# Products of one weight unit: all eight with the high parts, then all eight with the low parts

## The chip, the cores and the metric

The kernel runs on one NeuronCore of a Trainium2 chip. The metric is the device time of one execution in microseconds (us). An engine is named as in the profile: PE multiplies matrices, PEld is its weight load (which can run beside a product), DVE and ACT work on vectors, POOL does a few odd jobs, SP issues the DMAs.

## The reference

A two-layer encoder over 256 frames and a width of 2048. What matters here are the products with large weight matrices, all in float32:

```python
u = rms_norm(h, a_norm_g);  proj = u @ a_w_in          # q, k, v and a forget gate
h = h + forgetting_attention(q, k, v, logf) @ a_w_out
h = h + relu(rms_norm(h, g) @ w1)**2 @ w2              # 2048 -> 8192 -> 2048
kv = rms_norm(h, kv_norm_g) @ kv_w                     # shared keys and values
q = rms_norm(rms_norm(h, b_norm_g) @ b_w_q)            # layer 2: own queries
h = h + chunked_relbias_attention(q, k, v, rel) @ b_w_out
h = h + relu(rms_norm(h, g) @ w1)**2 @ w2
```

## The kernel before

**Split operands.** Weights and activations are split into a high part (rounded to the type `fp32r`) and a low part (the rest). A product of two such numbers is formed as high x high + high x low + low x high; low x low is left out. An activation tile `x[k]` holds the high parts of 128 features of all 256 frames in columns 0 to 255 and their low parts in columns 256 to 511.

**Units.** The weights stream from memory in 768 units of 128 x 1024 numbers (512 KB). For each, `issue` has SP start a DMA into `raw` (L94, 4 buffers), ACT write `hi` (L96, 3 buffers) and DVE write `lo = raw - hi` (L97, 3 buffers). `fetch` keeps two units ahead of the one that is handed out.

**Two ways to use a unit.** In `panel_a` (192 units: queries, keys and values of both layers) the activations are the stationary operand and the weights stream through as the moving one: twelve products of 512 columns for each unit (L179 to L181). In `panel_b` (576 units: both output projections and both MLPs) the weights are stationary. A unit holds four row blocks (`j`) of two 128-column blocks (`i`). `unit_b` forms, for each of these eight tiles, a pair:

- L191: `hi` tile stationary, all 512 columns of `x[k]` moving. The result, 128 x 512, goes to the accumulator bank `ps[i]`.
- L192: the `lo` tile of the same place stationary, the 256 high columns of `x[k]` moving, added to the first 256 columns of the same bank.

Every product is preceded by a load of its own 128 x 128 stationary tile, so a unit has 16 loads and 16 products. Below, L191's products are called wide and L192's narrow.

**Panels.** Four units fill the two banks `ps[0]`, `ps[1]` of a panel (16 values of `k`). There are four accumulator banks, so in the MLPs the next panel has two banks of its own; the output projections take two panels together (`group=2`) and use all four. A finished bank goes to `evac`: `residual` (L228, L229, both DVE), or `act` of the MLP (L389 to L396, ACT and DVE), after which it may be overwritten. The last panel of all ends in `store`, which adds to `h` and sends it out (L448).

**Order on the engines.** The tile framework fixes each engine's instruction order when the kernel is built, and adds the semaphore waits. After each unit `run_fill` takes one entry of a list of small jobs (attention, the sums for the norms); `Stats.reduce` at L149 is one, four products with only 2 moving columns.

Of the kernel before, what the change touches and what calls it, by code (L numbers as in the profile page):

```python
# [15 lines left out]
P = 128  # L16
T = 256
NB = T // P
D = 2048
KT = D // P  # L20
# [10 lines left out]
UB = UN // 256  # L31
# [4 lines left out]
def trunk(ctx: ExitStack, tc: tile.TileContext, xT, gs, hg, bf, wgate, w_in, w_oa, w1a, w2a,  # L36
          w_kv, w_qb, w_ob, w1b, w2b, rel, out):
    nc = tc.nc
    V, S, G, TE = nc.vector, nc.scalar, nc.gpsimd, nc.tensor
# [67 lines left out]
    def run_fill():  # L107
        if fill:
            for f in fill.popleft():
                f()  # L110
# [73 lines left out]
            evac(b, ps[b])  # L184

    def unit_b(ps, hi, lo, x, u):
        for i in range(2):
            for j in range(UB):
                k = u * UB + j
                c = j * 256 + i * P  # L190
                TE.matmul(ps[i], hi[:, c : c + P], x[k], start=k == 0, stop=False)  # L191
                TE.matmul(ps[i][:, :T], lo[:, c : c + P], x[k][:, :T], start=False, stop=k == KT - 1)  # L192
        run_fill()

    def panel_b(x, evac, n, group=1):
        for n0 in range(0, n, group):
            ps = [[ps_acc.tile([P, 512], F32, name="acc") for _ in range(2)] for _ in range(group)]
            for u in range(KT // UB):
                for q in range(group):
                    hi, lo = fetch()  # L200
                    unit_b(ps[q], hi, lo, x, u)
            for q in range(group):
                for i in range(2):
                    evac(2 * (n0 + q) + i, ps[q][i])
# [75 lines left out]
    def qkv_tile(name):  # L280
        return qkv.tile([P, GH, T], F32, name=name)
# [5 lines left out]
            else:  # L287
                fill.append(it)

# [1 line left out]
    st0 = Stats("a")  # L291
    x = []

# [78 lines left out]
    for g in range(NG):  # L372
        q, k, v = qkv.tile([P, GH, T], F32, name="q", bufs=4), qkv_tile("k"), qkv.tile([P, NB, 512], F32, name="v")
# [40 lines left out]
    st2f = st2.flip()  # L414
    add_fill([[], [lambda: st2.reduce(True)], [lambda: st2f.reduce(True)]])

# [1 line left out]
    qs = []  # L418
    for g in range(NG):
        q = qkv.tile([P, GH, T], F32, name="q", bufs=4)  # L420
# [13 lines left out]
    for g in range(NG):  # L434
        k, v = qkv_tile("k"), qkv.tile([P, NB, 512], F32, name="v")
# [73 lines left out]
```

## Time and profile before

| | before |
|---|---|
| time, median of 3 runs | 2217.13 us (2215.26 to 2217.21) |
| profiled execution, first to last instruction | 2213.9 us |
| PE busy | 2207.1 us |
| PEld busy | 1911.9 us |
| DVE busy | 1371.1 us |
| ACT busy | 1097.4 us |
| granted PE clock | 1.000 |
| wide products L191 | 4608, 392 ns each as recorded |
| narrow products L192 | 4608, 280 ns each as recorded |
| loads of both | 9216, 187 and 189 ns each as recorded |

The profile gives for the profiled execution only its span, 2213.9 us; the median of the runs is 3.2 us above it, which is taken as what lies around the span. Products overlap: a recorded duration runs from a product's start to the modelled end of its last result, while the next product has long begun. What one product costs is therefore read from start to start, and is called its slot below.

### The profile page before, as it was taken

To read this page: it belongs to the slowest core of one execution; us is meant where nothing else is said; L and a number is where in the kernel's file an instruction comes from. 1 tells how busy PE (TensorE), PEld (TensorE's weight loads), DVE (VectorE), ACT (ScalarE), POOL (GpSimd) and SP (SyncE) were. 2 spreads that over 40 slices of the span, in tenths; PEclk is the share of its full clock that TensorE was granted. 3 is DMA by queue.
4 is the path that set the end of the run, shared out by engine and by line. 5 is a ranking of instruction groups with operands and counts; after the bars stand their busy time and mean duration, and the time that the engine had idled before them with its cause. 6 is when DMAs were issued, how large, how long until landed. Compare 5 with 4: busy or idle time off the path is not lost.

```text
span 2213.9 us, 31170 instructions
## 1 busy us (share of the span) xinstructions
PE 2207.1 (100%) x12084; PEld 1911.9 (86%) x12084; DVE 1371.1 (62%) x2011; ACT 1097.4 (50%) x1578; POOL 42.5 (2%) x53
## 2 busy tenths in 40 slices
PE   9999999999999999999999999999999999999999
PEld 7888888888888888888888888888888888888888
DVE  6665557665665566566765555667656655655665
ACT  5554555553454454355554555545534534544543
POOL 1000000000000000000000000000000000000000
PEclk9999999999999999999999999999999999999999
DMA  6555555555555555555555555455555555555564
GB/s 224 206 182 173 179 178 184 190 191 190 191 190 191 190 191 190 190 190 190 190 183 184 178 173 170 162 190 190 190 189 189 189 190 190 190 189 189 190 205 155
DMA packets 118819, 414.32 MB, mean 187 GB/s; under 512 B 13312, under 2 KB 19600, under 8 KB 118672
## 3 DMA queue, kind: packets, MB, share of 16 engines
q1 hardware_dynamic: 118672, 412.34, 56.5%
q8 instruction: 94, 1.54, 0.3%
q14 instruction: 53, 0.43, 0.1%
HBM read 410.17 MB, written 2.12 MB: 186 GB/s over the span
## 4 chain that ended last, share of the span: by engine, by line
PE 98%; DMA 1%; DVE 0%; ACT 0%; issue 0%; SPq 0%; POOL 0%; ACTq 0%; DVEq 0%
PE acc L191 47%; PE acc L192 25%; PE acc L179 8%; PE acc L181 8%; PE acc L180 8%; PE s L234 1%; PE po L262 1%; PE pt L223 1%; DMA raw<-in_w_in 0%; PE pt L256 0%; PE s L233 0%; PE po L263 0%; DMA bias<-cd 0%; PE s L331 0%; DVE lo L97 0%
## 5 line engine op out<-in xcount | busy, mean ns | idle before, releaser
L191 PE MATMUL acc<-act,hi 128*128 128x512 f32 x4608 | 1599.4, 392 | 0.0
L97 DVE TENSOR_TENSOR lo<-raw,hi 128x1024 fp32r<-128x1024 f32 (+1 forms) x770 | 938.3, 1221 | 730.4 <-ACT hi L96 729.1
L96 ACT ACTIVATE hi<-raw 128x1024 fp32r<-128x1024 f32 (+1 forms) x770 | 815.5, 1059 | 1028.3 <-PE acc L191 769.3
L192 PE MATMUL acc<-act,lo 128*128 128x256 f32 x4608 | 1288.6, 280 | 0.0
L191 PEld LDWEIGHTS acc<-act,hi 128*128 128x128 f32 x4608 | 862.0, 187 | 189.8
L192 PEld LDWEIGHTS acc<-act,lo 128*128 128x128 f32 x4608 | 870.3, 189 | 0.0
L179 PE MATMUL acc<-hi,act 128*128 128x512 f32 x768 | 311.1, 406 | 1.3 <-ACT act L120 1.1
L180 PE MATMUL acc<-lo,act 128*128 128x512 f32 x768 | 299.4, 390 | 0.6 <-DVE lo L97 0.5
L181 PE MATMUL acc<-hi,act 128*128 128x512 f32 x768 | 299.9, 391 | 0.0
L181 PEld LDWEIGHTS acc<-hi,act 128*128 128x128 f32 x768 | 144.0, 188 | 31.8 <-DVE act L121 0.5
L180 PEld LDWEIGHTS acc<-lo,act 128*128 128x128 f32 x768 | 144.5, 188 | 29.7 <-DVE lo L97 2.0
L179 PEld LDWEIGHTS acc<-hi,act 128*128 128x128 f32 x768 | 144.4, 188 | 29.6 <-ACT act L120 1.9
L229 DVE TENSOR_TENSOR h<-acc,h 128x256 f32<-128x256 f32 x160 | 67.0, 423 | 4.9
L228 DVE TENSOR_TENSOR h<-acc,h 128x256 f32<-128x256 f32 x160 | 65.8, 415 | 5.2 <-PE acc L192 5.2
L389 ACT ACTIVATE tb<-acc 128x256 f32<-128x256 f32 x128 | 47.9, 374 | 29.3 <-PE acc L192 29.3
L395 ACT ACTIVATE act<-a 128x256 fp32r<-128x256 f32 x128 | 52.7, 412 | 2.0
L390 DVE TENSOR_TENSOR tb<-acc,tb 128x256 f32<-128x256 f32 x128 | 53.4, 417 | 0.1
L396 DVE TENSOR_TENSOR act<-a,act 128x256 fp32r<-128x256 f32 x128 | 53.4, 418 | 0.0
L393 ACT ACTIVATE a<-tb 128x256 f32<-128x256 f32 x128 | 51.4, 401 | 0.0
L216 DVE TENSOR_TENSOR qn<-acc,rn 128x512 f32<-128x512 f32 x32 | 22.1, 691 | 37.4 <-POOL rn L214 37.4
L120 ACT ACTIVATE act<-h,gsb 128x256 fp32r<-128x256 f32 x80 | 38.6, 496 | 6.9 <-DVE h L229 6.8
L214 POOL TENSOR_TENSOR rn<-vv,mhalf 128x4 f32<-128x4 f32 x32 | 32.7, 1021 | 404.6 <-DVE vv L212 404.6
(113 smaller groups left out, 603.0 us busy)
## 6 DMA issues: line engine op xcount, KB each, us to landing
raw<-in_w1a SPq DMA_DIRECT2D x128, 512.0 KB, 3.3
raw<-in_w2a SPq DMA_DIRECT2D x128, 512.0 KB, 3.3
raw<-in_w1b SPq DMA_DIRECT2D x128, 512.0 KB, 3.3
raw<-in_w2b SPq DMA_DIRECT2D x128, 512.0 KB, 3.6
raw<-in_w_in SPq DMA_DIRECT2D x94, 512.0 KB, 3.4
raw<-in_w_kv SPq DMA_DIRECT2D x64, 512.0 KB, 3.4
raw<-in_w_oa SPq DMA_DIRECT2D x32, 512.0 KB, 4.2
raw<-in_w_qb SPq DMA_DIRECT2D x32, 512.0 KB, 3.3
```

The lines of the kernel that those rows point to most:

```text
L96: S.activation(hi[:, c], raw[:, c], AF.Copy)
L97: V.tensor_tensor(lo[:, c], raw[:, c], hi[:, c].bitcast(F32), op=ALU.subtract)
L179: TE.matmul(ps[b], xh, wh, start=k == 0, stop=False)
L180: TE.matmul(ps[b], xh, wl, start=False, stop=False)
L181: TE.matmul(ps[b], xl, wh, start=False, stop=k == KT - 1)
L191: TE.matmul(ps[i], hi[:, c : c + P], x[k], start=k == 0, stop=False)
L192: TE.matmul(ps[i][:, :T], lo[:, c : c + P], x[k][:, :T], start=False, stop=k == KT - 1)
L228: V.tensor_tensor(h[m], ps[:, :T], h[m], op=ALU.add)
L229: V.tensor_tensor(h[m], ps[:, T:], h[m], op=ALU.add)
L390: V.tensor_tensor(tb, ps[:, :T], tb, op=ALU.add)
L395: S.activation(t[:, :T], a, AF.Copy)
L396: V.tensor_tensor(t[:, T:], a, t[:, :T].bitcast(F32), op=ALU.subtract)
```

## The change

Inside a unit the loop over the parts moves outside. The same sixteen loads and products run, with the same operands, first the eight wide ones (bank 0, then bank 1), then the eight narrow ones (bank 0, then bank 1). The flags that open and close an accumulation follow.

```diff
     def unit_b(ps, hi, lo, x, u):
-        for i in range(2):
-            for j in range(UB):
-                k = u * UB + j
-                c = j * 256 + i * P
-                TE.matmul(ps[i], hi[:, c : c + P], x[k], start=k == 0, stop=False)
-                TE.matmul(ps[i][:, :T], lo[:, c : c + P], x[k][:, :T], start=False, stop=k == KT - 1)
+        for w, cols in ((hi, 2 * T), (lo, T)):
+            for i in range(2):
+                for j in range(UB):
+                    k = u * UB + j
+                    c = j * 256 + i * P
+                    TE.matmul(ps[i][:, :cols], w[:, c : c + P], x[k][:, :cols], start=w is hi and k == 0,
+                              stop=w is lo and k == KT - 1)
         run_fill()
```

In the changed kernel both kinds of product stand on L192, and lines below it are one higher (L228 becomes L229).

## The prediction

> **What bounds the kernel now.** I read the page first: the busy times, then the chain of waits that ended last.
>
> ```profile
> PE 2207.1 (100%) x12084; PEld 1911.9 (86%) x12084; DVE 1371.1 (62%) x2011; ACT 1097.4 (50%) x1578; POOL 42.5 (2%) x53
> PE 98%; DMA 1%; DVE 0%; ACT 0%; issue 0%; SPq 0%; POOL 0%; ACTq 0%; DVEq 0%
> PE acc L191 47%; PE acc L192 25%; PE acc L179 8%; PE acc L181 8%; PE acc L180 8%; PE s L234 1%; PE po L262 1%; PE pt L223 1%; DMA raw<-in_w_in 0%; PE pt L256 0%; PE s L233 0%; PE po L263 0%; DMA bias<-cd 0%; PE s L331 0%; DVE lo L97 0%
> ```
>
> PE makes up 98% of the chain, and 72% is the pair that the change takes apart. Then the waits of PE, all of them:
>
> ```profile
> PE pt L72 <- DVE mhalf L74: 1.2, 1, 1.2
> PE acc L179 <- ACT act L120: 1.1, 2, 0.6
> PE acc L180 <- DVE lo L97: 0.5, 1, 0.5
> PE acc L179 <- ACT hi L96: 0.2, 1, 0.2
> ```
>
> That is 3.0 us in total, at the start and in `panel_a`; `unit_b` waits for nothing. So there is no waiting to win in it, and the question is only what a product costs in one order and in the other. The timeline inside the first MLP (start, duration, engine) shows one pair, and the product eight pairs later:
>
> ```profile
> 1000.05 0.39 PE L191 MATMUL acc<-act,hi 128*128 128x512 f32 x1
> 1000.05 0.19 PEld L192 LDWEIGHTS acc<-act,lo 128*128 128x128 f32 x1
> 1000.28 0.28 PE L192 MATMUL acc<-act,lo 128*128 128x256 f32 x1
> 1000.28 0.19 PEld L191 LDWEIGHTS acc<-act,hi 128*128 128x128 f32 x1
> 1000.39 0.39 PE L191 MATMUL acc<-act,hi 128*128 128x512 f32 x1
> ...
> 1002.82 0.39 PE L191 MATMUL acc<-act,hi 128*128 128x512 f32 x1
> ```
>
> Eight pairs take 2.77 us. Over all units without a fill job the trace's starts give 2773.3 ns, within 1 ns, so 346.7 ns a pair. Each load starts with the product before its own, never earlier: one tile waits behind the active one. A narrow slot thus already holds a whole load (that of the next wide product) in every pair. For wide products in a row, `panel_a`:
>
> ```profile
> 1150.11 0.39 PE L179 MATMUL acc<-hi,act 128*128 128x512 f32 x1
> ...
> 1152.83 0.39 PE L179 MATMUL acc<-hi,act 128*128 128x512 f32 x1
> ```
>
> Twelve slots of 512 columns in 2.72 us: 226.7 ns. A pair less that is 346.7 - 226.7 = 120.0 ns for a narrow slot. The two differ by 106.7 ns for 256 columns, or 0.4167 ns a column; 226.7 - 512 x 0.4167 leaves 13.3 ns, and 120.0 - 256 x 0.4167 leaves 13.3 ns. So one rule, 13.3 ns a product plus 0.4167 ns a column, gives both, whether wide follows wide or narrow.
>
> **The change part by part.** *Wide in a row*: 8 x 226.7 = 1813.3 ns, with `panel_a` as the row for it. *Narrow in a row*: the trace has no two of them in sequence. Their slot cannot be under the streaming, 106.7 ns. What could lengthen it is the load: two loads 120 ns apart, each recorded with 189 ns, overlap. The nearest row for loads in close sequence is L149, products of 2 columns whose pace only the loads set, in the timeline at the end of an output projection:
>
> ```profile
> 407.96 0.28 PE L192 MATMUL acc<-act,lo 128*128 128x256 f32 x1
> 407.96 0.53 PEld L149 LDWEIGHTS pt<-ones,sqm 128*128 128x128 f32 x4
> 408.08 0.50 PE L149 MATMUL pt<-ones,sqm 128*128 128x2 f32 x4
> 408.41 0.19 PEld L191 LDWEIGHTS acc<-act,hi 128*128 128x128 f32 x1
> 408.44 0.47 PE L191 MATMUL acc<-act,hi 128*128 128x512 f32 x1
> 408.52 0.19 PEld L192 LDWEIGHTS acc<-act,lo 128*128 128x128 f32 x1
> ```
>
> Six loads start between 407.96 and 408.52. The first sits in a narrow slot of 120 ns; after that they come at 108, 112, 111 and 112 ns (0.11 between the last two lines), the last interval with an fp32r tile that is being loaded. So loads can follow one another every 112 ns, though each is recorded for 188: the rest is latency that overlaps. 112 is below 120, so a run of narrow products keeps 8 ns in hand. Bounds for its slot: 106.7 and 188 ns; I take 120.0, since the row that times loads alone lies under it. Then the narrow run is 8 x 120.0 = 960.0 ns, the unit 1813.3 + 960.0 = 2773.3 ns, and 576 units change by 0.
>
> The Trainium skill (TensorE: Matmul & The Clock Gate, section LDWEIGHTS) gives a load as columns / 1.2 ns, an estimated 106.7 ns for 128 columns, which is exactly what 256 moving columns take: a run of narrow products would sit at the point where load and stream tie. The measured 112 is 5 ns longer, and by either figure the sum is the same zero.
>
> *Handing over units.* `hi` is free for ACT after the eighth product, 1.81 us into the unit, instead of after the fifteenth (2.65 us); `lo` at the unit's end in both. `lo` is first needed 1.81 us into a unit instead of 0.23. The L191 and L192 starts against the ends of L96 and L97 show `hi` ready at least 3.7 us early (mostly 4.4), `lo` at least 2.2 (mostly 3.4). Both margins can only grow by this; cost 0, and 0 gain, as PE waits for neither. What is queued behind the moved wait for `lo` on PE, the narrow run, has 1.6 us more. ACT frees `raw` earlier, so SP issues the same DMAs no later; the order of SP's and POOL's instructions as built does not change.
>
> *Banks.* Bank 0 is finished 4 narrow slots (0.48 us) before the unit's end instead of eight pairs less (1.39 us): 0.91 us later. Bank 1 ends as before. In the built order DVE takes the first halves of both banks' `residual` before the second ones. Such a delay, passed to the next conversions, meets the 2.2 us above. In the output projections, where four banks are all in use, a bank is overwritten one panel-unit (2.77 us) or more after its completion, against four L228/L229 of 0.34 to 0.46 us and one L97 of 1.23: covered. At the ends of phases the sums for L149 were done at 407.55 and used at 408.08, 0.53 us in hand; some of it may be used up, 0 to 0.5 us at each of four places, I take 0.
>
> *The tail.* The last L229 of `h15` starts at 2210.86 and ends at 2211.28; then come the store's issue and its landing, to 2213.9. After the change two `residual`s of 0.34 to 0.46 us an instruction crowd behind the last product, and two stores of 0.34 us issue behind one another: between 0 and 0.9 us, I take 0.5.
>
> Sum: 2213.9 + 0 + 0.5 = 2214.4 us of span, and with the 3.2 us around it 2217.6. A change under 0.2% (4.4 us, about what a measurement of this kernel can tell from none) is called no change; that is 4.4 us / (576 x 7) = 1.1 ns on each narrow slot that follows a narrow one.
>
> **Rivals.** *A, faster: the recorded starts are the true slots.* From start to start the trace has 230.5 ns for a wide product before a narrow one and 116.5 ns for a narrow one before a wide one, not 226.7 and 120.0. If mixing widths costs a wide slot 3.8 ns and a narrow one really takes 116.5, the unit becomes 7 x 226.7 + 230.5 + 8 x 116.5 = 2749.4 ns, 23.9 less, times 576 is 13.8 us: 2203.8. For it: the rows as they stand. Against it: the narrow slot before L149 above, 407.96 to 408.08, is 120, and the sum of the pair fits one rule without a remainder; I read the 3.5 ns as where the start is recorded.
>
> *B, slower: narrow runs become bound by their loads.* In the run, load follows load with no wide slot between them. If the 13.3 ns of a product were to begin only when its tile is in, at the pace of the L149 loads, a slot would be 111.5 + 13.3 = 124.8 ns, 4.8 more; 7 x 576 x 4.8 = 19.4 us: 2237.0 us. If overlapping loads were not possible at all, 188 ns a slot would make it 274 us more. It decides from 121.1 ns on. For it: nothing in the trace tests two narrow fp32r slots in sequence, and each load there is still recorded as running when the next begins. Against it: a narrow slot holds a whole load already today, from the same starting point, and the first L149 rows keep their pace. The skill says of PE's queue (same page, step 1 of section Step-by-step) that it pulls loads ahead of products in flight when they target the background buffer. Were that several loads deep, today's wide slots would give narrow ones a reserve that the run uses up; the rows, with no load ahead by more than one, speak against it.
>
> *C: the change doesn't do what it says.* The builder could interleave the products again. The instruction order as built has 576 runs of eight wide and 576 of eight narrow ones, so this is out.
>
> **Chances.** No change 0.64: every slot but one kind has its own row. A 0.11, and 0.01 for anything else that gains: 0.12 faster. B at 4.8 ns or less 0.16, B beyond that 0.05, late banks that reach PE by over 4 us 0.03: 0.24 slower. The range goes from A's time to B's, 2203 to 2237: 0.64, about half to two thirds of A (0.06) and of B up to its price (0.13), some 0.83 in all. The likeliest case alone spans 2213 to 2222.
>
> **What would show it.** In the profile after: wide starts 0.227 us apart, narrow starts 0.120 apart, a unit of 2.773 us, PE waiting as little as before. B would show narrow starts 0.122 or more apart with a load at each; A a unit near 2.749; late banks a wait of the first wide product of a unit for DVE. A narrow slot off 120 by over 1.1 ns makes the prediction wrong.

## The result and the profile after

The changed kernel takes 2229.38 us, median of 3 runs (2228.19 to 2229.68), against 2217.13: 12.25 us more, a ratio of 1.0056 with a 95% interval of 1.0038 to 1.0074. By the bound of 0.2% it is slower; "no change" was the likeliest case of the prediction, and it is the case that did not happen. The time lies in the stated range, but only by luck: the upper end came from rival B, whose mechanism was not the one at work.

The page of the changed kernel, span, busy times and the chain that ended last:

```profile
span 2227.9 us, 31234 instructions
...
PE 2219.0 (100%) x12084; PEld 1920.1 (86%) x12084; DVE 1367.7 (61%) x2011; ACT 1090.7 (49%) x1578; POOL 44.4 (2%) x53
...
PE 97%; DMA 1%; DVE 1%; issue 0%; ACT 0%; SPq 0%; POOL 0%; DVEq 0%; ACTq 0%
PE acc L192 72%; PE acc L181 7%; PE acc L179 7%; PE acc L180 7%; DMA bias<-cd 1%; PE po L263 1%; PE pt L224 1%; PE s L235 1%; DVE lo L97 0%; PE pt L257 0%; DMA raw<-in_w_in 0%; PE po L264 0%; PE s L234 0%; DMA h<-in_xT 0%; PE s L332 0%
```

PE is busy 11.9 us longer with the same 12084 products, at a granted clock of 1.000. What PE waits for, all of it:

```profile
PE acc L179 <- ACT act L120: 1.8, 2, 1.6
PE po L263 <- DVE act L267: 1.3, 2, 0.8
PE pt L72 <- DVE mhalf L74: 1.2, 1, 1.2
PE acc L180 <- DVE lo L97: 0.5, 1, 0.5
```

Still no wait in `unit_b`: the time is in the products themselves. The timeline in the first MLP (products of one kind in sequence are merged: start of the first, time to the end of the last, number):

```profile
1000.27 1.12 PE L192 MATMUL acc<-act,lo 128*128 128x256 f32 x8
...
1001.23 2.00 PE L192 MATMUL acc<-act,hi 128*128 128x512 f32 x8
...
1003.07 1.11 PE L192 MATMUL acc<-act,lo 128*128 128x256 f32 x8
...
1004.02 0.63 PE L192 MATMUL acc<-act,hi 128*128 128x512 f32 x2
```

Read from start to start, the wide run takes 1.84 us (1001.23 to 1003.07) where 1.813 were forecast, the narrow run 0.95 where 0.960 were. The trace's starts give a unit of 2793.3 ns instead of 2773.3, within 1 ns in nearly all units without a fill job. Product by product (medians of each place, ns; the sum is that of the means):

| place in the run | 1 | 2 | 3 | 4 | 5 | 6 | 7 | 8 | sum |
|---|---|---|---|---|---|---|---|---|---|
| wide, after | 233 | 236 | 228 | 233 | 231 | 227 | 227 | 227 | 1840.8 |
| narrow, after | 113 | 119 | 120 | 120 | 120 | 120 | 120 | 120 | 952.5 |

From the third on, the narrow products come at 120 ns, as forecast. The loss is in the first five wide products after a narrow run: together 27.5 ns over 226.7 each. The first two narrow slots are together 7.5 ns short of 120 each, so 20 ns are left.

**Where the 12 us are.** 576 units x 20.0 ns = 11.5 us. The one stretch of each layer with nothing else in it, 253 units of an MLP, goes from 701.62 to 706.68 us: 5.06 us, or 20.0 ns a unit, twice. The spans differ by 14.0 us. Of the other 2.5, the tail behind the last product is 0.4 (3.83 to 4.19 us), and 2.2 lie ahead of the first wide product (310.4 and 312.6 us), in a part that the change does not touch; in the kernels of the experiments this start lies anywhere between 310.3 and 312.4 whatever the order, so it is not counted to the change.

### The profile page after: what moved, and what is told of

Its sections match the earlier page's. It is cut to its first block, busy times and chain, and to the rows that moved or that the text cites. A ratio compares the mean times of both kernels' runs of the same rounds, so it can differ in the third digit from the quotient of the medians.

```text
span 2227.9 us, 31234 instructions
## 1 busy us (share of the span) xinstructions
PE 2219.0 (100%) x12084; PEld 1920.1 (86%) x12084; DVE 1367.7 (61%) x2011; ACT 1090.7 (49%) x1578; POOL 44.4 (2%) x53
## 4 chain that ended last, share of the span: by engine, by line
PE 97%; DMA 1%; DVE 1%; issue 0%; ACT 0%; SPq 0%; POOL 0%; DVEq 0%; ACTq 0%
PE acc L192 72%; PE acc L181 7%; PE acc L179 7%; PE acc L180 7%; DMA bias<-cd 1%; PE po L263 1%; PE pt L224 1%; PE s L235 1%; DVE lo L97 0%; PE pt L257 0%; DMA raw<-in_w_in 0%; PE po L264 0%; PE s L234 0%; DMA h<-in_xT 0%; PE s L332 0%
## 5 line engine op out<-in xcount | busy, mean ns | idle before, releaser
L192 PE MATMUL acc<-act,hi 128*128 128x512 f32 x4608 | 1155.1, 392 | 0.0
L192 PEld LDWEIGHTS acc<-act,hi 128*128 128x128 f32 x4608 | 828.3, 189 | 148.5
L192 PEld LDWEIGHTS acc<-act,lo 128*128 128x128 f32 x4608 | 628.6, 190 | 45.0
L192 PE MATMUL acc<-act,lo 128*128 128x256 f32 x4608 | 642.5, 282 | 0.0
L229 DVE TENSOR_TENSOR h<-acc,h 128x256 f32<-128x256 f32 x160 | 67.9, 425 | 78.8 <-PE acc L192 73.7
L230 DVE TENSOR_TENSOR h<-acc,h 128x256 f32<-128x256 f32 x160 | 60.3, 414 | 0.0
```

The lines of the kernel that those rows point to most:

```text
L192: TE.matmul(ps[i][:, :cols], w[:, c : c + P], x[k][:, :cols], start=w is hi and k == 0, stop=w is lo and k == KT - 1)
L229: V.tensor_tensor(h[m], ps[:, :T], h[m], op=ALU.add)
L230: V.tensor_tensor(h[m], ps[:, T:], h[m], op=ALU.add)
```

## The experiments

Each kernel ran once with a profile, beside a run of the kernel before (2215.98, 2216.77 and 2216.30 us in the three groups). The unit's length is read from the trace's starts, where it repeats within 1 ns, and decides more finely than the times. "By rule" is 13.3 ns a product plus 0.4167 ns a column. W and N stand for wide and narrow products.

| kernel | sequence in `unit_b` | unit by rule, ns | measured | over the rule | time, us |
|---|---|---|---|---|---|
| before | 512, 256 in turn | 2773.3 | 2773.3 | 0 | 2217.13 |
| after | 8 x 512, 8 x 256 | 2773.3 | 2793.3 | 20.0 | 2229.38 |
| g2 | 2 and 2 | 2773.3 | 2786.7 | 13.3 | 2225.23 |
| g4 | 4 and 4 | 2773.3 | 2806.7 | 33.3 | 2236.59 |
| alt16 | 16 and 16 over two units | 2773.3 | 2783.3 | 10.0 | 2222.72 |
| banks | 8 and 8, banks in turn | 2773.3 | 2793.3 | 20.0 | 2229.64 |
| w5n2 | W5 N2 W1 N2 W1 N2 W1 N2 | 2773.3 | 2806.7 | 33.3 | 2237.16 |
| w2n5 | W2 N5 W2 N1 W2 N1 W2 N1 | 2773.3 | 2806.7 | 33.3 | 2236.50 |
| n288_pairs | 512, 288 in turn | 2880.0 | 2906.7 | 26.7 | 2294.96 |
| n288_runs | 8 x 512, 8 x 288 | 2880.0 | 2901 to 2905 | 21 to 25 | 2292.55 |
| n384_runs | 8 x 512, 8 x 384 | 3200.0 | 3266.7 | 66.7 | 2500.74 |
| n512_runs | 16 x 512 | 3626.7 | 3626.7 | 0 | 2707.97 |
| n128_pairs | 512, 128 in turn | 2346.7 | 2720.0 | 373.3 | 2188.56 |
| n128_runs | 8 x 512, 8 x 128 | 2346.7 | 2746.7 | 400.0 | 2210.33 |

In the last two the loads set the pace of the narrow products, so the rule of columns does not apply to them.

### Shorter runs: g4 and g2

The first line put in is that of g4, the second that of g2; the other two are common.

```diff
-        for w, cols in ((hi, 2 * T), (lo, T)):
-            for i in range(2):
-                for j in range(UB):
+        for grp in ([(i, j) for j in range(UB)] for i in range(2)):      # g4
+        for grp in ([(i, j), (i, j + 1)] for i in range(2) for j in (0, 2)):   # g2
+            for w, cols in ((hi, 2 * T), (lo, T)):
+                for i, j in grp:
```

> Groups of four: for each bank four wide products, then the four narrow ones (two runs of each kind in a unit instead of one). Theory L (a narrow product that follows a narrow one costs 2.9 ns more than 120, because its load paces it; 7 x 2.9 = 20 ns a unit in the changed kernel): 6 x 2.9 ns, a unit of 2790.5 ns against 2793.3 after and 2773.3 before, about 1.6 us less than after over 576 units. Theory S (the cost, 20 ns, is paid at each return from a narrow run to wide products): two returns, 2813 ns a unit, about 11.5 us more than after.

> Groups of two: two wide products, then their two narrow ones, four times in a unit. Theory L: four narrow products follow a narrow one, 4 x 2.9 = 11.4 ns, a unit of 2784.8 ns. Theory S: four returns, up to 80 ns, a unit of up to 2853 ns.

Measured: 2806.7 and 2786.7 ns. In the timeline of g4 (PE's lines alone), four wide products take 0.93 us (4 x 226.7 = 0.907) and their four narrow ones 0.48 or 0.47:

```profile
1000.00 1.09 PE L192 MATMUL acc<-act,hi 128*128 128x512 f32 x4
1000.93 0.64 PE L192 MATMUL acc<-act,lo 128*128 128x256 f32 x4
1001.41 1.09 PE L192 MATMUL acc<-act,hi 128*128 128x512 f32 x4
1002.34 0.63 PE L192 MATMUL acc<-act,lo 128*128 128x256 f32 x4
1002.81 0.40 PE L192 MATMUL acc<-act,hi 128*128 128x512 f32 x1
```

In g4 fewer narrow products in sequence cost more, not less, and their slots are not longer than 120: theory L, a price on each of them, falls, though its 2784.8 for g2 is only 1.9 ns off. S has the direction for g4 but not its size (33.3, not 40), and g2 is far below its bound of 80.

### Longer runs: alt16

```diff
-        for w, cols in ((hi, 2 * T), (lo, T)):
+        parts = ((hi, 2 * T), (lo, T))
+        for w, cols in parts if u % 2 == 0 else parts[::-1]:
 ...
-                              stop=w is lo and k == KT - 1)
+                              stop=w is hi and k == KT - 1)
```

> Every second unit of a panel runs its narrow products first, so that two units in sequence make runs of 16 of a kind. Theory R (each round from wide products to narrow ones and back costs an amount that grows with the length of the runs and levels off: 0 for runs of one, 3.3 ns for two, 16.7 for four, 20 for eight): one round in two units, 10 ns a unit, 2783.3 ns on average, half the loss of the changed kernel. Theory P (the loss belongs to places in the unit, its banks and tiles, and not to the length of runs): 2793 ns as in the changed kernel.

Measured: 5566.7 ns for two units, 20 ns over the rule, as R said. The timeline shows a run of each kind:

```profile
1002.37 2.08 PE L193 MATMUL acc<-act,lo 128*128 128x256 f32 x16
1004.28 3.82 PE L193 MATMUL acc<-act,hi 128*128 128x512 f32 x16
1007.94 1.24 PE L193 MATMUL acc<-act,lo 128*128 128x256 f32 x9
```

Sixteen narrow products, each with its load, take 1.91 us: after the first two, every start is 120 ns behind the one before. Then again only the first five wide products are late (about 233, 236, 228, 232, 231), and the other eleven keep 226.7. So 120 ns is a pace that narrow products hold, and next to 256 columns the loss belongs to the return to wide ones.

### Other places in the unit: banks

```diff
-        for w, cols in ((hi, 2 * T), (lo, T)):
-            for i in range(2):
-                for j in range(UB):
+        for grp in ([(i, j) for j in range(UB) for i in range(2)],):
+            for w, cols in ((hi, 2 * T), (lo, T)):
+                for i, j in grp:
```

> Runs of eight as in the changed kernel, but successive products alternate between the two accumulator banks, and two in sequence stream the same x[k]. Theory R: nothing changes, 2793.3 ns a unit with the first five wide starts late. Theory P: another sum, and another pattern of starts.

Measured: 2793.3 ns, and the same starts to the ns (233, 236, 228, 233, 231, 227 and so on). Which bank is written, and whether two products share their moving tile, makes no difference.

### Which run sets the price: w5n2 and w2n5

The code is shortened; the banks alternate, as in banks.

```diff
+        for n, (p, j, i) in enumerate(seq):       # seq: "WWWWWNNWNNWNNWNN" or "WWNNNNNWWNWWNWWN"
+            w, cols = (hi, 2 * T) if p == "W" else (lo, T)
+            TE.matmul(ps[i][:, :cols], w[:, c : c + P], x[k][:, :cols], ...
```

> A unit in the pattern W5 N2 W1 N2 W1 N2 W1 N2 (W wide, N narrow, banks alternating): no narrow run is over two, one wide run is five. If the length of the narrow run sets the cost: four returns of 3.3 ns as in g2, 2786.7 ns a unit. If the wide run sets it: one return of about 18 ns and three of none, 2791 ns.

> A unit in the pattern W2 N5 W2 N1 W2 N1 W2 N1: one narrow run of five, no wide run over two. If the narrow run sets the cost: one return of about 18 ns and three of none, 2791 ns a unit. If the wide run sets it: four of 3.3 ns, 2786.7 ns.

Measured: 2806.7 ns for both. Neither reading holds. Four narrow runs of two cost 33.3 ns in w5n2 and 13.3 in g2, and four wide runs of two cost 33.3 in w2n5 and 13.3 in g2, so the length of one of the two kinds of run does not set the price. A price that depends on the whole pattern is left, and no run here gives its law.

### Other widths: n288_runs, n128_runs, n384_runs, n512_runs

Only the width of the narrow products is changed in the changed kernel, to 288, 128, 384 or 512 columns; the order is the same:

```diff
-        for w, cols in ((hi, 2 * T), (lo, T)):
-            for i in range(2):
-                for j in range(UB):
+        for grp in ([(i, j) for i in range(2) for j in range(UB)],):
+            for w, cols in ((hi, 2 * T), (lo, 384)):
+                for i, j in grp:
```

> The changed kernel with narrow products of 288 columns instead of 256 (32 columns of low x low are added). By the rule of 13.3 ns a product plus 0.4167 ns a column a narrow slot is 133.3 ns and a unit 2880.0. Theory L: the stream is longer than the load's pace of some 122.9 ns, so nothing is added: 2880 ns. Theory S: 2900 ns.

> The changed kernel with narrow products of 128 columns (the low weight products of frames 128 to 255 are left out). By the rule of columns alone a narrow slot would be 66.7 ns and a unit 2346.7. Theory L: the slot can't fall under the load's pace in a run, some 122.9 ns, so a unit stays near 2790 ns. Theory S: a load takes less, 112 ns as at L149, so a unit of 1813.3 + 8 x 112 = 2709 ns plus up to 20.

> The changed kernel with narrow products of 384 columns (128 columns of low x low are added): by the rule a slot of 173.3 ns and a unit of 8 x 226.7 + 8 x 173.3 = 3200.0. Theory W (the loss comes from going back from narrow to wide products, whatever the load has in hand): still above 3200 by 5 to 25 ns. Theory B, in the form that short slots in the run leave loads late: with 173 ns for a load of 112 nothing can be late, 3200 ns.

> The changed kernel with all sixteen products at 512 columns (all of low x low is added), so only the tiles change from high to low and back. Theory W: no change of width, no loss, 16 x 226.7 = 3626.7 ns a unit. If the change of tile costs (another buffer, another engine's wait): 3646 ns.

At 288 columns a narrow product has more time than its load needs under theory L, and yet the unit is 21 to 25 ns over the rule. At 384 columns a slot of 173.3 ns stands against a load of 112, and the loss is the largest but for 128 columns, 66.7 ns, over theory W's own 25:

```profile
1001.43 2.01 PE L192 MATMUL acc<-act,hi 128*128 128x512 f32 x8
1003.28 1.58 PE L192 MATMUL acc<-act,lo 128*128 128x384 f32 x8
1004.70 2.01 PE L192 MATMUL acc<-act,hi 128*128 128x512 f32 x8
```

Eight wide products in 1.85 us and eight of 384 in 1.42 (8 x 173.3 = 1.387): 36.7 ns of the loss are in the wide products and 30.0 in those of 384 columns, so the return to wide ones is not the only place. This is the end of rival B as it was stated: at the L149 pace of 112 ns the loads have 60 ns to spare. One form of it stays open. A load is recorded with 187 to 192 ns and starts 2 to 5 ns after the product before its own (some 50 ns in part of the runs with 128 columns), so in each narrow slot from 112 to 173 ns it is recorded as running into its own product, and only in slots of 512 columns it is not. No width between 384 and 512 was run, which would tell a slot shorter than the recorded load from a mere difference of width. Against it: the kernel before has such loads in every narrow slot and loses nothing, and in the changed kernel the loads of the second to fifth wide products start 225 to 234 ns ahead of them. With 512 columns throughout, runs of high and low tiles alternate as in the changed kernel, and nothing is lost:

```profile
1000.20 1.98 PE L192 MATMUL acc<-act,hi 128*128 128x512 f32 x8
1002.01 1.98 PE L192 MATMUL acc<-act,lo 128*128 128x512 f32 x8
1003.82 0.39 PE L192 MATMUL acc<-act,hi 128*128 128x512 f32 x1
```

1.81 us a run, all starts 226 or 227 ns apart. So neither the change from `hi` to `lo` tiles nor their hand-over costs; in these runs the loss comes only where widths differ. The run with 128 columns took 2210.33 us and 2746.7 ns a unit: after the first two, its narrow starts come at 110 to 114 ns, which is the load's pace of L149, nothing like 122.9 (theory L), but the whole is 38 ns over the 2709 that the pace alone gives. Its time holds 4.5 us more in which PE waits for `residual` on DVE in the output projections.

### Other widths in pairs: n288_pairs and n128_pairs

```diff
-        for w, cols in ((hi, 2 * T), (lo, T)):
-            for i in range(2):
-                for j in range(UB):
+        for grp in ([(i, j)] for i in range(2) for j in range(UB)):
+            for w, cols in ((hi, 2 * T), (lo, 288)):
+                for i, j in grp:
```

(or `P` for 128; this gives the order of before, one wide and one narrow product in turn.)

> The order of before with narrow products of 288 columns. Theory W as stated for runs of one: no loss, 8 x (226.7 + 133.3) = 2880 ns a unit, against 2901 to 2905 for the same products in runs of eight. If 256 next to 512 columns is a happy case of its own, more than 2880.

> The order of before with narrow products of 128 columns (the low products of frames 128 to 255 are left out). Measures a load against a short slot without a run: by streaming alone 8 x (226.7 + 66.7) = 2346.7 ns a unit; if a narrow slot can't fall under the load's 112 ns, 8 x (226.7 + 112) = 2709 ns. Runs of eight took 2746.7.

Measured: 2906.7 ns with 288 columns, 26.7 over the rule, no better than the runs of eight (the whole kernel even 2.4 us slower). So theory W's "no loss for runs of one" was a property of 512 next to 256, not of pairs. With 128 columns a unit takes 2720 ns, a little over 8 x (226.7 + 112), and the kernel 2188.56 us. Read from start to start, though, the slots are 280 ns (wide) and 60 (narrow):

```profile
1000.13 0.22 PE L192 MATMUL acc<-act,lo 128*128 128x128 f32 x1
1000.13 0.19 PEld L192 LDWEIGHTS acc<-act,hi 128*128 128x128 f32 x1
...
1000.19 0.44 PE L192 MATMUL acc<-act,hi 128*128 128x512 f32 x1
1000.24 0.19 PEld L192 LDWEIGHTS acc<-act,lo 128*128 128x128 f32 x1
1000.47 0.22 PE L192 MATMUL acc<-act,lo 128*128 128x128 f32 x1
```

The narrow tile's load starts 51 ns after the wide product, 108 ns behind the load before it. So it is the spacing of two loads that stretches the pair, and the time shows in the wide slot: only the pair's sum can be read.

## Why the prediction was wrong in its likeliest case

- *What bounds the kernel*: right. PE is all of the chain before and after, nothing in `unit_b` waits, and the answer lay in the slots.
- *Narrow in a row, 8 x 120.0 = 960.0 ns*: this was the step with no row of its own, bounded from 106.7 to 188, and it held: 120 ns a slot, sixteen in sequence in alt16.
- *Wide in a row, 8 x 226.7 = 1813.3 ns*: this is the term that failed. It measured 1840.8, 27.5 more (20 net of the short first narrow slots). Its row came from a stretch of `panel_a`, where every neighbour is 512 columns wide too. The row was used as if a product's slot depended on its own width alone. "One rule gives both, whether wide follows wide or narrow" was drawn from two sequences, 512 throughout and 512/256 in turn. n512_runs shows the first and the kernel before the second to be free of loss; of the ten other sequences with narrow products of 256 columns or more, the changed kernel's among them, none is as fast as the rule. The trace of the kernel before had a row nearer to the case: after the fill jobs in `panel_a`, whose products are of other kinds and widths, the slots of 512 columns are late too. After four products of 128 columns (L223) it shows

```profile
1141.65 0.60 PE L223 MATMUL pt<-ident,qn 128*128 128x128 f32 x4
1142.01 0.47 PE L179 MATMUL acc<-hi,act 128*128 128x512 f32 x1
1142.32 0.39 PE L180 MATMUL acc<-lo,act 128*128 128x512 f32 x1
...
1144.63 0.39 PE L181 MATMUL acc<-hi,act 128*128 128x512 f32 x1
```

Ten slots from 1142.32 to 1144.63 take 2.31 us instead of 2.267. The row that the prediction used starts at 1150.11, 5 us behind the last fill job, where the slots have settled. Over the kinds of fill job there, ten such slots are late by 22 to 44 ns together (medians). So a loss of that size at each return to wide products stood in the trace and was priced at nothing.

- *Rival A* (faster, starts read as slots): out. The narrow slot is 120 in sequence. The prediction's own reading of the 3.5 ns, a shift in where a start is recorded, stays unshown: in the changed kernel the last wide slot before a narrow run is 226.7, not 230.5.
- *Rival B* (narrow runs bound by their loads): the sign was right, the mechanism not. Narrow starts are not 122 or more apart, the loss of the changed kernel appears in its wide products, and with 384 columns, where at 112 ns a load no load is late, it is larger. It was priced 19.4 us; the change cost 12.25 for another reason. The prediction's sign of being wrong, a narrow slot off 120 by over 1.1 ns, watched the wrong kind of product.
- *Rival C*, and late banks: out. The order ran as built; PE's waits in `unit_b` stay at none. (Bank 0 used to be finished four pairs before the unit's end, where the prediction says eight; its 1.39 us are those of four.) `hi` is now ready at least 4.3 us ahead of its use (mostly 5.3), `lo` at least 2.4 (mostly 5.9): the margins grew, as forecast.
- *The tail*: forecast 0.5 us, measured 0.4. What lies around the span was taken as 3.2 us from the median; the profiled run after (2229.68 with a span of 2227.9) shows 1.8.

What makes a product slower after products of another width is not settled. Shown not to be the cause: waits, a load's pace of 112 ns, the banks and tiles, the step from `hi` to `lo`. Conversions on ACT and DVE are out as well: in the changed kernel the last one ends at 2217.0, and the last unit, well behind it, has the same 1.84 us wide run (2221.04 to 2222.88):

```profile
2221.04 2.00 PE L192 MATMUL acc<-act,hi 128*128 128x512 f32 x8
2222.88 1.11 PE L192 MATMUL acc<-act,lo 128*128 128x256 f32 x8
```

The wide slots in question mostly come from one small set (224, 228, 231, 233, 236; up to 241 in w2n5), 231 to 232 on average, about 5 over the settled 226.7, and the set is the same after fill jobs in the kernel before. After runs of eight or more of 256 columns they settle in five products; next to 288, 128 and 384 columns they do not settle in eight. That reads like two streams that have to fall into step again, loads and products, but no run here shows these inside PE, and none leaves the loads out, so it stays a reading.

The Trainium skill (TensorE: Matmul & The Clock Gate, section Back-to-back issue gap) gives the spacing of a single warm product, apart from any stream of loads and products, as columns / 2.4 + 2.5 ns. The runs here, with a load for every product, show 213.3 + 13.3 ns at 512 columns, and no one fixed amount fits all the mixed sequences.

## What to carry to other kernels

On a PE that never waits, the order of products is a cost of its own: read the slot of a product with the neighbours it will have, and do not take it from a row with others. Look for such a row in the trace at hand, behind a fill job for instance, before calling a step known. A sequence in which every product has the same width, or the strict turn of 512 and 256 columns, ran without loss here; every other mixture tried lost time, so a mixture of fp32r widths should be measured by the length of its unit before it is kept. If runs of 512 and 256 columns must be formed for another reason, 8 and 8 and 16 and 16 both lost 20 ns a round, so the longer round halved the loss; other lengths do not follow this.

## What the hardware showed that was not expected

- Equal work in another order costs 0 to 33 ns in a unit of 2773, and not in order of run length: 1, 2, 4, 8, 16 in sequence give 0, 13.3, 33.3, 20 and 10 ns a unit.
- 32 columns more on each narrow product cost 133.3 ns a unit in pairs (2773.3 to 2906.7) where their streaming accounts for 106.7.
- Loads of 128 x 128 fp32r tiles held a pace of 110 to 114 ns beside products of 128 columns in n128_runs, while each is recorded with 187 to 192 ns.
- Ten wide slots of `panel_a` right behind four L223 products took 2.31 us in the kernel before, 43 ns more than ten settled ones.
